# First MLP of a two-layer trunk: half 1 of its input turned once per token block, the Strassen-like forms made behind the turn

## The chip, the cores and the metric

The kernel runs on one core of one Trainium2 chip. The metric is the time of one execution on the device in microseconds (us). Before the change three runs gave 2055.06, 2055.20 and 2062.24 us; the median is 2055.2 us. Lower is better.

## The reference

The input x has 1024 tokens of 1024 channels in float32. There are two layers. The first mixes tokens with a gated linear recurrence, the second with a causal convolution; each mixer is followed by a layer norm, an MLP with squared ReLU and another layer norm. Cut to the place that matters here, the end of the first mixer and the first MLP:

```python
for i in range(DEPTH):
    ...
    x = layer_norm(DEEPNORM_ALPHA * x + mix, ln_mix_g[i], ln_mix_b[i])
    ff = jnp.square(jax.nn.relu(x @ ffn_w1[i])) @ ffn_w2[i]
    x = layer_norm(DEEPNORM_ALPHA * x + ff, ln_ffn_g[i], ln_ffn_b[i])
```

ffn_w1 is 1024 x 4096 and ffn_w2 is 4096 x 1024. The change concerns how x, the output of the first layer norm, is brought into the shape in which the product with ffn_w1 takes it.

## The kernel before

**Precision.** Every float32 operand is split into a high part (rounded to fp32r by a copy) and a low part (the rest), and a product is three matmuls, high x high, high x low and low x high (`product`, line 335). `split` (line 1042) makes the parts: a ScalarE copy for the high one, a VectorE subtraction for the low one.

**Seven products for eight.** The large products go by a scheme with seven products of half-sized blocks. The tokens are cut in two halves of 512 (half 0 and 1) and the channels in two halves of 512 (k = 0 and 1). Write x00, x10 for half 0 and channels 0 or 1, and x01, x11 for half 1. The MLP then needs seven forms of its input, kept transposed (channels on the partitions) and split, in `xf[1]` to `xf[7]` (line 1144): form 1 is x00, 2 is x10, 3 is x11, 5 is x00 - x01, 7 is x11 - x01, 6 is -(form 5) - x11 and 4 is -(form 6) - x10. `forms_of` (line 1119) makes forms 5, 6, 7 and 4 from four blocks. Seven forms of each weight block go with them; `Forms.unit` (line 130) loads four raw tiles of 128 x 1024 and makes the weights' forms from them in the order of `ORDER` (line 45): 1, 2, 6, 5, 7, 3, 4.

**The stage of the change (lines 1132 to 1178).** The output projection of the first mixer is computed block by block: four blocks t of 128 tokens in each half, two column halves n each, 24 matmuls a product. VectorE adds each product to y (`y[half]`, the residual), and behind n = 1 `x1_block` (line 1154) normalises the block. For half 0 two background jobs ("chores") turn the block: `turn` (line 1096) transposes four 128 x 128 pieces on TensorE into one PSUM bank of the ring `aux` (banks 3 and 4) and splits them from there into `xf[1]` and `xf[2]`. For half 1 `forms_of` makes tiles t for forms 5 and 6 (ring `ts`, two tiles of 2 KB per partition at 200 and 202 KB) and for form 4 (ring `t4s`, 212 to 218 KB) while tokens are still on the partitions, and each form is turned and split on its own. `keep` (line 1104) stores y to DRAM for the residual after the MLP. `x1_late` (line 1417) does what is left, form 3 and form 7 (ring `t7s` at 48 and 50 KB), during the first products of the MLP.

**The first MLP (lines 1411 to 1445).** Four early products (`up.form` at lines 1426 to 1430: the first two forms of the weight blocks c = 0 and c = 1) take weights that are loaded ahead (`early`, line 1141). Then the loop over c takes forms from `fw` (line 1413): weight slots at 144, 152, 48, 112 and 120 KB, raw tiles at 192, 196, 200 and 204 KB, sums at 160 and 164 KB. `Up` (line 1186) keeps squared ReLU outputs in `hr` at 168 and 176 KB and their forms in `ht` at 184 to 190 KB.

**What sets the order.** A chore is popped by every `product` (line 342, `bg.chore`). All buffers are views of one space at addresses written out in KB, so a view waits until those that lie there before it are free. Up to line 1038 the order on every engine is the one of the program; behind it the queues are ordered by the scheduler of the tile framework with its own timeline (line 1920), so the order in the trace differs from the program's in places.

Of the kernel before, what the change touches and what calls it, by code (L numbers as in the profile page):

```python
# [8 lines left out]
F32 = mybir.dt.float32  # L9
# [3 lines left out]
ALU = mybir.AluOpType  # L13
PSUM = bass.MemoryType.PSUM

P = 128
D = 1024
# [3 lines left out]
HT = 512  # L21
NTB = HT // P
# [141 lines left out]
class LateForms(Forms):  # L164

    turned = True
# [102 lines left out]
def body(ctx, tc, d, out):  # L269
    nc = tc.nc  # L270
# [9 lines left out]
    def view(kb, shape, dt=F32, name="t"):  # L280
        at, top = int(kb * 1024), KBYTES * 1024
        if at < edge[0]:
            if edge[0] < top:
                space.tile([P, (top - edge[0]) // 4], F32, name="gap")
            edge[0] = 0
        if at > edge[0]:
            space.tile([P, (at - edge[0]) // 4], F32, name="gap")
        edge[0] = at + (prod(shape) + 7) // 8 * 32
        return space.tile([P, *shape], dt, name=name)

    def ring(kbs, shape, name, dt=F32):
        return Ring([view(kb, shape, dt, name) for kb in kbs])

    def run(kb, n, size):
        return [kb + i * size for i in range(n)]

    def slots(kbs, name):
        return ring(kbs, (2, 1024), name, F32R)

    def raws(kbs, name="raw"):  # L300
        return ring(kbs, (1024,), name)
# [21 lines left out]
    bg = Background()  # L323
    vector = Clocked(nc.vector, bg.dve, vector_cost)
    tensor = Clocked(nc.tensor, bg.pe, tensor_cost)
# [6 lines left out]
    def aux():  # L332
        return rings["aux"]().rearrange("p (a b) -> p a b", a=NTB)
# [40 lines left out]
    ident = cst.tile([P, P], F32, name="ident")  # L374
    wide_t, rows = (HT,), (NTB, P)

    XF, VS, VO = {}, {}, {}
    x00, x10, x01, x11, t6 = [view(kb, (4, HT), F32, "xr") for kb in run(112, 5, 8)]
# [663 lines left out]
    def split(hi, lo, ps, scale=None):  # L1042

        if scale is None:
            nc.scalar.copy(out=hi, in_=ps)
            vector.tensor_tensor(out=lo, in0=ps, in1=hi.bitcast(F32), op=ALU.subtract)
        else:
            nc.scalar.activation(hi, ps, AF.Copy, scale=scale)
            vector.scalar_tensor_tensor(out=lo, in0=ps, scalar=scale, in1=hi.bitcast(F32), op0=ALU.mult, op1=ALU.subtract)
# [7 lines left out]
    def gain(kb, name, layer):  # L1057
        return vec(kb, f"{name}_g", layer), vec(kb + 4, f"{name}_b", layer)
# [12 lines left out]
    def moments(yt):  # L1071
        bs = stat.tile([P, 2, 6], F32, tag="bs", name="bs")
        for j in range(2):
            half_stats(bs, yt, j)
        mv = rstd_of(bs)
        return mv[:, 0:1], mv[:, 3:4]
# [14 lines left out]
    def norm(yt, g, b):  # L1091
        mu, rs = moments(yt)
        vector.scalar_tensor_tensor(out=yt, in0=yt, scalar=mu, in1=g, op0=ALU.subtract, op1=ALU.mult)
        vector.scalar_tensor_tensor(out=yt, in0=yt, scalar=rs, in1=b, op0=ALU.mult, op1=ALU.add)

    def turn(yt, xt, t, k0, nk):

        for k in range(0, nk, 4):
            pt = aux()
            for j in range(4):  # L1100
                tensor.transpose(pt[:, j, :], yt[:, (k0 + k + j) * P : (k0 + k + j + 1) * P], ident)
            split(xt[:, 0, k : k + 4, t * P : (t + 1) * P], xt[:, 1, k : k + 4, t * P : (t + 1) * P], pt)

    def keep(half, t, src):
        nc.sync.dma_start(out=kept[half][t], in_=src)
# [10 lines left out]
    def blocks(name, layer, c):  # L1116
        return [d[name][layer, c, q] for q in range(4)]

    def forms_of(x, out, only=(5, 6, 7, 4)):

        t = {i: out(i) for i in only}
        if 5 in only:
            vector.tensor_tensor(out=t[5], in0=x[0][0], in1=x[0][1], op=ALU.subtract)
            vector.scalar_tensor_tensor(out=t[6], in0=t[5], scalar=-1.0, in1=x[1][1], op0=ALU.mult, op1=ALU.subtract)
        if 7 in only:
            vector.tensor_tensor(out=t[7], in0=x[1][1], in1=x[0][1], op=ALU.subtract)
        if 4 in only:
            vector.scalar_tensor_tensor(out=t[4], in0=t[6], scalar=-1.0, in1=x[1][0], op0=ALU.mult, op1=ALU.subtract)
        return t
# [3 lines left out]


    g, b = gain(192, "ln_mix", 0)
    y = [view(160 + 16 * h, (NTB, D), F32, "y") for h in range(2)]
    for half in range(2):
        for t in range(NTB):
            nc.sync.dma_start(out=y[half][:, t], in_=d["x"][half * HT + t * P : half * HT + (t + 1) * P])
    ts, t4s = ring(run(200, 2, 2), wide_t, "t"), ring(run(212, 4, 2), wide_t, "t4")  # L1140
    early = [Slots(nc, vector, slots((204,), "fw"), raws((0,))), Slots(nc, vector, slots((112, 120), "fw"), raws((96, 100)))]
    early.append(Slots(nc, vector, slots((144,), "fw"), raws((152,))))

    xf = {i: view(kb, (2, 4, HT), F32R, f"x1f{i}") for i, kb in ((6, 0), (5, 16), (3, 32), (1, 64), (2, 80), (7, 96), (4, 128))}
    early[0].plan(blocks("w1q", 0, 0)[:1])
    early[1].plan([blocks("w1q", 0, 0)[1], blocks("w1q", 0, 1)[0]])
    early[2].plan(blocks("w1q", 0, 1)[1:2])
    yb = [[[y[n][:, t, k * HT : (k + 1) * HT] for n in range(2)] for k in range(2)] for t in range(NTB)]
    tt = {}

    def x1_form(t, i, src=None, k=0):
        turn(tt[t][i] if src is None else src, xf[i], t, k, 4)

    def x1_block(half, t):
        norm(y[half][:, t, :], g, b)
        if half == 0:
            bg.chores += [lambda: x1_form(t, 1, y[0][:, t, :]), lambda: x1_form(t, 2, y[0][:, t, :], 4)]
            return
        tt[t] = forms_of(yb[t], lambda i: (t4s if i == 4 else ts)(), (5, 6, 4))
        keep(0, t, y[0][:, t, :])  # L1160
        if t < NTB - 1:
            bg.chores += [lambda: x1_form(t, 6), lambda: x1_form(t, 5)]

    for half in range(2):
        for t, n in early_out + ((0, 1), (1, 1), (3, 0), (2, 1), (3, 1)) if half == 0 else [(t, n) for t in range(NTB) for n in range(2)]:
            ps = acc()
            if half or (t, n) not in early_out:
                product(ps, wide(oT[half], t, ws[n]))
            yv = y[half][:, t, n * HT : (n + 1) * HT]
            vector.scalar_tensor_tensor(out=yv, in0=yv, scalar=ALPHA, in1=ps, op0=ALU.mult, op1=ALU.add)  # L1170
            if n == 1:
                if half == 1 and t == 0:
                    early[0].ahead(1)
                x1_block(half, t)
                if half == 0 and t:
                    bg.chore()
# [232 lines left out]
            nc.sync.dma_start(out=raw, in_=d[name][at])  # L1409
            staged.append((name, at))  # L1410

    t7s = ring((48, 50), wide_t, "t7")
    fw = Forms(nc, vector, slots((144, 152, 48, 112, 120), "fw"), raws(run(192, 4, 4)), raws(run(160, 2, 4), "sum"), spare, 3, range(44))
    fw.todo = [[(blocks("w1q", 0, c), 2 if c < 2 else 0)] for c in range(NFC)]
    up = Up()

    def x1_late(t):
        turn(y[1][:, t, :], xf[3], t, 4, 4)
        tt[t].update(forms_of(yb[t], lambda i: t7s(), (7,)))
        x1_form(t, 7)  # L1420
        keep(1, t, y[1][:, t, :])

    late_forms = [lambda t=t: x1_late(t) for t in range(NTB)]
    bg.chores += [lambda: None] + late_forms[:1] + [lambda: x1_form(NTB - 1, 6), lambda: x1_form(NTB - 1, 5)] + late_forms[1:]
    bg.chores += [lambda t=t: x1_form(t, 4) for t in range(NTB)]
    up.form(0, 1, early[0].take(1)[0])
    up.form(0, 2, early[1].take(1)[0], late=True)
    up.form(1, 1, early[1].take(1)[0], ring((208, 210), wide_t, "c1"))
# [19 lines left out]
    y = [view(32 + 16 * h, (NTB, D), F32, "y") for h in range(2)]  # L1448
    fw = Slots(nc, vector, slots([112, 120, 144, 152, 128, 136, 168], "dw"), raws([192, 196, 200, 204, 160, 164], "dr"), spare, 6, range(10, 50))
    fh = Slots(nc, vector, slots([0, 8, 16, 24, 96, 104, 176], "dh"))  # L1450
    g, b = gain(184, "ln_ffn", 0)
# [61 lines left out]
    taken, turned, gate, normed = [0], [0], [None, [], None], [0]  # L1513
# [306 lines left out]
    y = [view(kb, (NTB, D), F32, "y") for kb in (88, 112)]  # L1820
    g, b = gain(184, "ln_ffn", 1)
# [102 lines left out]
```

## Time and profile before

| What | Value |
| --- | --- |
| Median of three runs | 2055.2 us |
| Span of the profiled execution | 2068.3 us |
| TensorE busy | 2031.0 us, 98% |
| VectorE busy | 1482.9 us, 72% |
| ScalarE busy | 1090.2 us, 53% |
| GpSimd busy | 388.4 us, 19% |
| Mean granted TensorE clock | 0.997 |
| Transposes of 128 x 128 between 440 and 570 us | 112 |
| First matmul of the first MLP (`ps<-x1f,fw`) | 519.7 us |

The profiled execution is one run of its own with a span of 2068.3 us from the first to the last instruction; nothing of the execution lies around that span in the trace, and it is longer than the median of the three timed runs. In a row of the profile, PE is TensorE's matmuls, PEld its weight loads, DVE VectorE, ACT ScalarE, POOL GpSimd and SPq the queue of SyncE, which issues DMA transfers. `out<-in` names the tiles written and read: ps is PSUM, x1f the seven forms `xf`, fw the weight forms, ident the identity matrix of a transpose, y the residual blocks, t the form tiles, raw and sum the raw weights and their sums. The bracket at the end of a timeline row gives how long the engine was idle before it and what ended that. A row with xN merges N instructions that follow each other.

### The profile page before, as it was taken

The numbers are of one execution on the slowest core, as the hardware profiler recorded it, in microseconds if no ns is written. First come the engines' busy times: TensorE is split into PE (matmuls) and PEld (weight loads), VectorE is DVE, ScalarE is ACT, GpSimd is POOL, SyncE is SP. The second block draws the span as 40 slices with busy tenths as digits, with TensorE's granted clock in tenths as the row PEclk, the third lists the DMA queues.
The fourth block names the chain that finished last, engine by engine and source line by source line (L and its number), as shares of the span: only waits on it lengthen the run. The fifth ranks groups of instructions, "written<-read, shape, count | busy, mean of one in ns | idle before, by whom it ended". The sixth has DMA issues, their size and how long they took to land. (4 is left out here: it accounts for less than half of the span.)

```text
span 2068.3 us, 29719 instructions
## 1 busy us (share of the span) xinstructions
PE 2031.0 (98%) x11192; PEld 1674.5 (81%) x11192; DVE 1482.9 (72%) x1976; ACT 1090.2 (53%) x1727; POOL 388.4 (19%) x387
## 2 busy tenths in 40 slices
PE   8999999999999999999999999999999999999998
PEld 7888777788888888888888888888878878888886
DVE  8698877877775666565567898889589666755556
ACT  5456555641464555444444776488625555343333
POOL 0112222111001000000001699079210000100002
PEclk9999999999999999999999999999999999999999
DMA  4778889852689786999998855587759778996542
GB/s 186 224 195 233 238 224 270 254 189 81 187 288 298 243 295 221 353 341 332 335 349 292 309 193 185 190 323 271 256 215 339 245 232 291 386 292 204 193 155 102
DMA packets 183944, 517.55 MB, mean 250 GB/s; under 512 B 17912, under 2 KB 49784, under 8 KB 182776
## 3 DMA queue, kind: packets, MB, share of 16 engines
q1 hardware_dynamic: 168312, 456.93, 62.6%
q0 software_dynamic: 15488, 58.72, 12.3%
q8 instruction: 87, 1.43, 0.3%
q14 instruction: 57, 0.47, 0.1%
HBM read 380.85 MB, written 201.85 MB: 282 GB/s over the span
## 5 line engine op out<-in xcount | busy, mean ns | idle before, releaser
L204 PE MATMUL ps<-dw,dh 128*128 128x512 f32 x2688 | 611.6, 389 | 1.9 <-ACT dh L72 1.1
L204 PEld LDWEIGHTS ps<-dw,dh 128*128 128x128 f32 x2688 | 504.1, 188 | 107.2 <-ACT dh L72 1.6
L204 PE MATMUL ps<-x1f,fw 128*128 128x512 f32 x1344 | 309.3, 390 | 2.3 <-DVE c L204 1.2
L204 PEld LDWEIGHTS ps<-x1f,fw 128*128 128x128 f32 x1344 | 251.1, 188 | 56.2 <-ACT c L1224 2.3
L204 PE MATMUL ps<-xf,fs 128*128 128x512 f32 x1008 | 249.3, 398 | 4.1 <-issue 1.9
L204 POOL TENSOR_TENSOR cb<-cb,prod 128x512 f32<-128x512 f32 x168 | 222.7, 1334 | 12.9 <-ACT prod L1555 2.3
L204 DVE TENSOR_TENSOR dh<-dh 128x1024 fp32r<-128x1024 f32 x112 | 136.4, 1222 | 117.3 <-ACT dh L72 117.1
L204 PEld LDWEIGHTS ps<-xf,fs 128*128 128x128 f32 x1008 | 184.5, 189 | 43.4 <-issue 2.1
L204 DVE SCALAR_TENSOR_TENSOR ps<-u,par,ps 128x512 f32<-128x512 f32 x296 | 206.2, 750 | 11.0 <-ACT ps L1567 9.5
L72 ACT CAST dh<-dh 128x1024 fp32r<-128x1024 f32 x112 | 117.4, 1051 | 163.7 <-DMA dh<-hf 163.7
L204 PE MATMUL ps<-xa,wa 128*128 128x512 f32 x864 | 203.1, 392 | 0.1
L204 PEld LDWEIGHTS ps<-xa,wa 128*128 128x128 f32 x864 | 160.3, 188 | 33.3 <-ACT ha L1289 0.3
L204 DVE TENSOR_TENSOR dw<-dr,dw 128x1024 fp32r<-128x1024 f32 x112 | 136.2, 1222 | 66.6 <-ACT dw L72 65.9
L72 ACT CAST dw<-dr 128x1024 fp32r<-128x1024 f32 x112 | 117.0, 1051 | 119.2 <-PE ps L204 100.2
L1555 ACT ACTIVATE prod<-u,par 128x512 f32<-128x512 f32 x168 | 119.8, 726 | 36.6 <-POOL cb L204 35.7
L518 POOL TENSOR_TENSOR mv<-mv,nhalf 128x1 f32<-128x1 f32 x32 | 43.3, 1355 | 407.6 <-DVE mv L204 407.6
L1408 POOL COPY next<-ss 128x1 f32<-128x1 f32 x38 | 21.2, 558 | 413.8 <-DVE spare L204 265.1
L204 PE MATMUL ps<-xb,wa 128*128 128x512 f32 x384 | 91.1, 393 | 0.0
L204 PE MATMUL ps<-w,oT 128*128 128x512 f32 x384 | 89.5, 391 | 1.3 <-ACT oT L932 0.8
L204 DVE TENSOR_TENSOR spare<-next,spare 128x1024 fp32r<-128x1024 f32 x38 | 46.5, 1224 | 60.6 <-ACT spare L1401 60.5
L204 PE MATMUL ps<-vw,xf 128*128 128x512 f32 x336 | 79.8, 399 | 6.0 <-ACT vw L435 5.2
L204 PEld LDWEIGHTS ps<-w,oT 128*128 128x128 f32 x384 | 71.5, 188 | 16.6 <-ACT oT L932 1.2
(236 smaller groups left out, 2959.6 us busy)
## 6 DMA issues: line engine op xcount, KB each, us to landing
wa<-ready SPq DMA_DIRECT2D x140, 512.0 KB, 5.5
dh<-hf SPq DMA_DIRECT2D x112, 512.0 KB, 5.3
sum_w<-in_w_dram POOLq DMA_DIRECT2D x40, 1024.0 KB, 10.9
ready<-spare SPq DMA_DIRECT2D x76, 512.0 KB, 4.6
raw<-in_w1q_dram SPq DMA_DIRECT2D x66, 512.0 KB, 4.4
dr<-sum_w SPq DMA_DIRECT2D x64, 512.0 KB, 5.7
hf<-ht SPq DMA_DIRECT2D x112, 256.0 KB, 4.9
dr<-in_w_dram SPq DMA_DIRECT2D x48, 512.0 KB, 5.3
```

The source lines that it names most:

```text
L72: self.nc.scalar.copy(out=slot[:, 0, c], in_=raw[:, c])
L204: return op(*args, **kw)
L518: nc.gpsimd.tensor_tensor(out=dst, in0=src, in1=nhalf[:, :n], op=ALU.pow)
L1408: nc.gpsimd.tensor_copy(out=raw[:, :1], in_=now)
L1555: nc.scalar.activation(tp, u[:, k : k + HT], AF.Copy, scale=tap(j, k))
```

## The change

Half 1's block is turned as it is, once: four transposes per channel half, eight per block. The forms are then made from the turned block in PSUM and from `xf[1]` and `xf[2]`, whose high and low parts are added up again.

- `x1_first` turns channels 0 of a block of half 1 (x01) and makes form 5 from `xf[1]` high, the turned block and `xf[1]` low; it splits it, and leaves x01 in its PSUM bank.
- `x1_second` turns channels 1 (x11), makes and splits form 6, copies x11 out of PSUM into `late_x[3]`, makes form 7 into `late_x[7]`, and form 4 into `late_x[4]`.
- `x1_late` splits forms 3, 7 and 4 from there, two channel groups of all 512 tokens (128 x 1024) at a time: six wide splits. They are chores of their own behind three empty ones, so that the first comes with the fourth early product.
- The two halves of y change places (half 0 at 176, half 1 at 160 KB); `late_x[3]` and `late_x[7]` take half 0's place at 176 and 184 KB once it is turned, `late_x[4]` takes 212 to 220 KB. `t4s` and `t7s` go. `keep` is called behind the norm for every block.

```diff
-    y = [view(160 + 16 * h, (NTB, D), F32, "y") for h in range(2)]
+    y = [view(160 + 16 * h, (NTB, D), F32, "y") for h in range(2)][::-1]
...
-    ts, t4s = ring(run(200, 2, 2), wide_t, "t"), ring(run(212, 4, 2), wide_t, "t4")
+    ts = ring(run(200, 2, 2), wide_t, "t")
+    late_x = {4: view(212, (4, HT), F32, "x4")}
...
-    def x1_form(t, i, src=None, k=0):
-        turn(tt[t][i] if src is None else src, xf[i], t, k, 4)
+    def of(x, t, i=slice(None)):
+        return x[..., t * P : (t + 1) * P] if i == slice(None) else x[:, i, :, t * P : (t + 1) * P]
+
+    def turned(yt, k0):
+        pt = aux()
+        for j in range(4):
+            tensor.transpose(pt[:, j, :], yt[:, (k0 + j) * P : (k0 + j + 1) * P], ident)
+        return pt
...
+    def x1_first(t):
+        s, pt = ts().rearrange("p (a b) -> p a b", a=4), turned(y[1][:, t, :], 0)
+        less(s, of(xf[1], t, 0).bitcast(F32), pt)
+        vector.tensor_tensor(out=s, in0=s, in1=of(xf[1], t, 1).bitcast(F32), op=ALU.add)
+        x1_split(5, t, s)
+        temp[t], x01[t] = s, pt
+
+    def x1_second(t):
+        s, pt = ts().rearrange("p (a b) -> p a b", a=4), turned(y[1][:, t, :], 4)
+        minus_both(s, temp[t], pt)
+        nc.scalar.copy(out=of(late_x[3], t), in_=pt)
+        less(of(late_x[7], t), of(late_x[3], t), x01[t])
+        x1_split(6, t, s)
+        x4 = of(late_x[4], t)
+        minus_both(x4, s, of(xf[2], t, 0).bitcast(F32))
+        less(x4, x4, of(xf[2], t, 1).bitcast(F32))
+
+    def x1_late(i, k):
+        split(xf[i][:, 0, k : k + 2], xf[i][:, 1, k : k + 2], late_x[i][:, k : k + 2])
...
     def x1_block(half, t):
         norm(y[half][:, t, :], g, b)
+        keep(half, t, y[half][:, t, :])
...
-        tt[t] = forms_of(yb[t], lambda i: (t4s if i == 4 else ts)(), (5, 6, 4))
-        keep(0, t, y[0][:, t, :])
+        if t == 0:
+            bg.done()
+            late_x.update({i: view(kb, (4, HT), F32, "xl") for i, kb in ((3, 176), (7, 184))})
         if t < NTB - 1:
-            bg.chores += [lambda: x1_form(t, 6), lambda: x1_form(t, 5)]
+            bg.chores += [lambda: x1_first(t), lambda: x1_second(t)]
...
-    t7s = ring((48, 50), wide_t, "t7")
...
-    late_forms = [lambda t=t: x1_late(t) for t in range(NTB)]
-    bg.chores += [lambda: None] + late_forms[:1] + [lambda: x1_form(NTB - 1, 6), lambda: x1_form(NTB - 1, 5)] + late_forms[1:]
-    bg.chores += [lambda t=t: x1_form(t, 4) for t in range(NTB)]
+    bg.chores += [lambda: None, lambda: x1_first(NTB - 1), lambda: x1_second(NTB - 1)] + [lambda: None] * 3
+    bg.chores += [lambda i=i, k=k: x1_late(i, k) for i in (3, 7, 4) for k in (0, 2)]
```

`split`, `turn`, `norm` and `keep` are unchanged; `minus_both(out, x, y)` is -x - y, `less` is x - y.

More of the change, by code (lines that the diff above doesn't have):

```diff
@@ L1147, in body @@
     early[2].plan(blocks("w1q", 0, 1)[1:2])
-    yb = [[[y[n][:, t, k * HT : (k + 1) * HT] for n in range(2)] for k in range(2)] for t in range(NTB)]
-    tt = {}
-    def x1_form(t, i, src=None, k=0):
-        turn(tt[t][i] if src is None else src, xf[i], t, k, 4)
+    temp, x01 = {}, {}
+    def of(x, t, i=slice(None)):
[5 more added lines that the diff above has]
+        return pt
@@ new lines, in less, with minus_both, x1_split @@
+    def less(out, x, y):
+        vector.tensor_tensor(out=out, in0=x, in1=y, op=ALU.subtract)
+    def minus_both(out, x, y):
+        vector.scalar_tensor_tensor(out=out, in0=x, scalar=-1.0, in1=y, op0=ALU.mult, op1=ALU.subtract)
+    def x1_split(i, t, src):
+        split(of(xf[i], t, 0), of(xf[i], t, 1), src)
+    def x1_first(t):
[4 more added lines that the diff above has]
+        temp[t], x01[t] = s, pt
@@ L1154, in x1_block @@
     def x1_block(half, t):
         norm(y[half][:, t, :], g, b)
+        keep(half, t, y[half][:, t, :])
         if half == 0:
-            bg.chores += [lambda: x1_form(t, 1, y[0][:, t, :]), lambda: x1_form(t, 2, y[0][:, t, :], 4)]
+            bg.chores += [lambda k=k: turn(y[0][:, t, :], xf[1 + k // 4], t, k, 4) for k in (0, 4)]
             return
-        tt[t] = forms_of(yb[t], lambda i: (t4s if i == 4 else ts)(), (5, 6, 4))
-        keep(0, t, y[0][:, t, :])
+        if t == 0:
+            bg.done()
+            late_x.update({i: view(kb, (4, HT), F32, "xl") for i, kb in ((3, 176), (7, 184))})
@@ L1415, in body @@
     up = Up()
[L1417 to L1421, printed above, removed]
-    late_forms = [lambda t=t: x1_late(t) for t in range(NTB)]
-    bg.chores += [lambda: None] + late_forms[:1] + [lambda: x1_form(NTB - 1, 6), lambda: x1_form(NTB - 1, 5)] + late_forms[1:]
-    bg.chores += [lambda t=t: x1_form(t, 4) for t in range(NTB)]
+    bg.chores += [lambda: None, lambda: x1_first(NTB - 1), lambda: x1_second(NTB - 1)] + [lambda: None] * 3
+    bg.chores += [lambda i=i, k=k: x1_late(i, k) for i in (3, 7, 4) for k in (0, 2)]
     up.form(0, 1, early[0].take(1)[0])
```

## The prediction

> **What bounds the kernel now.** I read the page's head first, then the granted clock, then TensorE's waits, then TensorE's timeline around the stage that the diff touches.
>
> ```profile
> span 2068.3 us, 29719 instructions
> PE 2031.0 (98%) x11192; PEld 1674.5 (81%) x11192; DVE 1482.9 (72%) x1976; ACT 1090.2 (53%) x1727; POOL 388.4 (19%) x387
> ```
> ```profile
> core 0: 2068.3 us, clock 0.997
> ```
> TensorE is busy 98% of the span at a clock of 0.997, so the clock is not in play, and 37 us of TensorE idle is all that waits can cost. An edit shortens the kernel only by taking instructions off TensorE or by closing part of those 37 us. The stage of the diff lies near a quarter of the span:
>
> ```profile
> core 0: us, PE busy (x) PEld busy (x) DVE busy (x) ACT busy (x) POOL busy (x), PEclk, DMA share, GB/s
> 500.00:520.00 20.00, 20.00 (x98) 16.76 (x97) 14.77 (x22) 2.34 (x4) 1.45 (x1) 1.00 0.30 93
> 520.00:540.00 20.00, 20.00 (x98) 16.65 (x97) 13.95 (x21) 10.23 (x16) 1.45 (x1) 1.00 0.49 170
> 540.00:560.00 20.00, 19.01 (x98) 15.73 (x97) 15.67 (x18) 10.86 (x18) 1.26 (x1) 1.00 0.71 212
> 560.00:580.00 20.00, 20.00 (x94) 16.32 (x94) 15.51 (x18) 11.35 (x18) 1.67 (x2) 1.00 0.82 193
> ```
> Here TensorE rests once, for about 1 us between 540 and 560; VectorE is busy 14 to 16 of 20 us and ScalarE at most 11. Behind 600 us the view of waits lists eleven reasons for which TensorE rests, the largest and the smallest being
>
> ```profile
> PE ps L204 <- ACT dh L72: 1.1, 1, 1.1
> PE ps L204 <- ACT z L1634: 0.2, 1, 0.2
> ```
> so none is over 1.1 us, all of them are under 12 us, and what is won at 500 to 570 us should reach the end.
>
> **What the change takes from TensorE.** Only the transposes of this stage:
>
> ```profile
> L204 PE MATMUL ps<-ident,t 128*128 128x128 f32 x64 | 9.3, 272 | 0.0
> L204 PE MATMUL ps<-ident,y 128*128 128x128 f32 x48 | 6.5, 272 | 0.0
> ```
> (The lines view from 440 to 570 us.) Before, every one of four token blocks has four transposes for each of the forms 6, 5, 7 and 4, made from tiles t (the 64), and for form 3 from y of half 1 (16 of the 48; the other 32 are half 0's and stay). After, a block of half 1 takes eight, four per half of D. So 64 + 16 become 32: 48 fewer. What one costs is not its 272 ns, which overlap, but the distance between starts:
>
> ```profile
> 495.39 1.03 PE L204 MATMUL ps<-ident,t 128*128 128x128 f32 x8
> 496.18 11.14 PE L204 MATMUL ps<-w,oT 128*128 128x512 f32 x48
> ...
> 526.17 0.60 PE L204 MATMUL ps<-ident,y 128*128 128x128 f32 x4
> 526.61 0.60 PE L204 MATMUL ps<-ident,t 128*128 128x128 f32 x4
> 526.96 8.20 PE L204 MATMUL ps<-x1f,fw 128*128 128x512 f32 x35
> ...
> 542.15 2.30 PE L204 MATMUL ps<-x1f,fw 128*128 128x512 f32 x9
> 545.43 3.91 PE L204 MATMUL ps<-x1f,fw 128*128 128x512 f32 x16 [0.99 <-DVE c L204]
> ...
> 558.45 0.60 PE L204 MATMUL ps<-ident,t 128*128 128x128 f32 x4
> 558.81 2.80 PE L204 MATMUL ps<-x1f,fw 128*128 128x512 f32 x11
> ```
> Eight delay the next matmul by 496.18 - 495.39 = 0.79 us, four by 558.81 - 558.45 = 0.36 us: 0.09 to 0.10 us each, so 48 are 4.3 to 4.7 us; I take 4.5. [...]
>
> In the timeline, 24 of the 80 transposes of half 1 stand before 519 us (24 also afterwards, of y instead of t), 24 between 526 and 545 (eight afterwards, the last block's) and 32 behind 545 (none afterwards). So 16 go ahead of the rest at 545.43, 1.5 us, and 32 behind it, 3.0 us.
>
> **What it adds to VectorE and ScalarE.** From the same lines view:
>
> ```profile
> L204 DVE TENSOR_TENSOR x1f<-ps,x1f 128x512 fp32r<-128x512 f32 x26 | 17.0, 681 | 11.2 <-ACT x1f L1045 11.2
> L204 DVE TENSOR_TENSOR fw<-raw,fw 128x1024 fp32r<-128x1024 f32 x6 | 7.2, 1214 | 1.7 <-ACT fw L72 1.7
> L204 DVE SCALAR_TENSOR_TENSOR t<-t,y 128x512 f32<-128x512 f32 x8 | 5.5, 683 | 0.0
> L204 DVE TENSOR_TENSOR t<-y 128x512 f32<-128x512 f32 x8 | 5.4, 687 | 0.1
> ```
> A block had four form operations and five split subtractions, nine of about 0.685 us. It gets three (first half) and five (second half), eight, with three of PSUM-reading and the rest of plain operands; the rows of both kinds agree (681 and 687 ns), so I price them alike. The six wide splits, 128x1024, are 1.21 us each. VectorE: 36 x 0.685 = 24.7 us before, 32 x 0.685 + 6 x 1.21 = 29.2 after, 4.5 more. In the loop over half 1, five operations per block become eight, 2.1 us more in a block of 507.16 - 495.39 = 11.77 us, of which VectorE now uses some 8.7 (14.77 of 20): 10.8 of 11.77. It fits, with 1 us left, so TensorE keeps its pace there, but the block's normalisation ends later. Behind 545 us the wide splits (7.3 us) replace some nine narrow ones (6.2 us): no difference. ScalarE gets three copies per block instead of five, and six wide ones of 1.05 us: about 1.6 us more on an engine that is half idle.
>
> **Edits that I cost at nothing.** The swapped places of y's halves and the earlier stores of kept:
>
> ```profile
> 423.36 6.54 SPq L1139 DMA_DIRECT2D y<-in_x_dram  x5
> 446.43 1.37 DVE L204 SCALAR_TENSOR_TENSOR y<-y,ps 128x512 f32<-128x512 f32 x2 [2.80 <-PE ps L204]
> ```
> y's last load leaves SyncE's queue at 429.9 us and its first reader runs at 446.43, after TensorE; half 0's new place is that of the recurrence's last tiles, free by then, so 16 us of matmuls cover it; without that cover a late load costs what it is late. The stores of kept are the same eight issues of 0.3 to 0.4 us, put behind each norm, and are read only by the down projection.
>
> **The wait that decides.** At 542.9 us (545.43 - 0.99 - 1.5) TensorE will be through with the four early products and wants the forms of the first full unit. All but one need raw[2] of four raw tiles. It lies at 200 KB (line 1413), over both t buffers (200 and 202, line 1140), so its load waits until t is free:
>
> ```profile
> 526.85 1.29 DVE L204 SCALAR_TENSOR_TENSOR y<-y,mv,ln_mix_b 128x1024 f32<-128x1024 f32 x1 [0.44 <-POOL mv L518]
> ...
> 528.65 1.28 DVE L204 TENSOR_TENSOR x1f<-ps,x1f 128x512 fp32r<-128x512 f32 x2
> ...
> 530.45 0.68 DVE L204 TENSOR_TENSOR c<-c,ps 128x512 f32<-128x512 f32 x1
> 531.05 1.41 DVE L204 SCALAR_TENSOR_TENSOR t<-t,y 128x512 f32<-128x512 f32 x2
> ...
> 540.06 1.22 DVE L204 TENSOR_TENSOR sum<-raw 128x1024 f32<-128x1024 f32 x1 [2.44 <-DMA raw<-in_w1q_dram]
> ```
> ```profile
> 536.30 6.47 SPq L135 DMA_DIRECT2D raw<-in_w1q_dram  x2
> ```
> ```profile
> 535.67 0.60 PE L204 MATMUL ps<-ident,t 128*128 128x128 f32 x4
> ```
> ```profile
> 535.63 1.26 ACT L1045 CAST x1f<-ps 128x512 fp32r<-128x512 f32 x2 [0.53 <-PE ps L204]
> ...
> 541.32 1.06 ACT L72 CAST fw<-sum 128x1024 fp32r<-128x1024 f32 x1 [1.63 <-DVE sum L204]
> ```
> Now: the last norm ends at 528.14, the t tiles that are turned are made by 531.7, the last transposes read them at 535.67 and after, until 536.27; the load leaves at 536.30, VectorE starts on it at 540.06 (3.76 later, having idled for it), ScalarE's cast of the sum ends at 542.4. From issue to usable weights are 6.1 us. Today TensorE then still has 2 us of product left, so this chain is just hidden.
>
> After: the norm ends at 528.1 plus 0 to 2.4 us (eight operations of block 2 where two splits and two seventh forms stood, some of them in gaps); I take 529.3. TensorE takes transposes up to 4 us behind their input (531.7 to 535.67 above): 3.5, so 532.8. But now t is read by VectorE, not TensorE, and is free only after the seventh of the block's eight operations: 0.4 for the transposes, 7 x 0.6 (two in 1.28, one in 0.68, so one every 0.6), one ScalarE copy between (0.6), two additions of early products ahead (1.3), 6.5 us, so 539.3. Issue, load, sum and cast: 539.4 + 6.1 = 545.5, against 545.43 today. The bounds: with the norm at 528.1, TensorE at once and nothing between, t is free at 533.3, the weights come at 539.5 and TensorE doesn't wait for them, so the restart is at 542.9; with the norm at 530.5 and 4 us to the transposes it is at 541.1 + 6.1 = 547.2. I expect TensorE to wait 2.6 us there: the 1.5 us of the 16 transposes and the old 0.99 us of rest become one longer wait.
>
> **Sum.** Ahead of the restart 0.0 (from -2.5 to +1.8), behind it -3.0: -3.0 us (-5.5 to -1.2) on the profiled span, 2068.3 to 2065.3. The runs shown have a median of 2055.2, 0.6% below that span, with the highest at 2062.24; the same 3.0 us, 0.15%, come off: 2052.2. A measurement of this kernel can tell about 0.5%, 10.3 us, from no change, so this would read as the same.
>
> **Rivals.**
> (A) The wait is hidden and all of it is won: 4.5 + 1.0 = 5.5 us, 2049.7. For it: slot 48 of the weight ring is no longer shared with the seventh forms' tiles, so the third form comes sooner. Against it: the load at 536.30 was already bare for 2.44 us on VectorE.
> (B) Slower than before: the same chain, but t is held so long that the restart comes after 548.4 us, where it has eaten the 3.0 us behind it as well; from there the kernel is a us slower for each us. If VectorE falls behind by 1 us in each of the loop's four blocks, the norm ends at 533.3, t is free at 543.3 and the restart at 549.5: 2056.3. With three of the wide splits ahead of the first sums, 3.6 us more: 2059.9. For it: VectorE at 10.8 of 11.77 us. Against it: TensorE rested nowhere in that loop, and its products have six PSUM banks (line 1132) to run ahead in.
> (C) A transpose costs TensorE its whole record: 48 x 0.272 = 13.1 us, 2042.1. Against it: eight of them in 0.79 us. [...]
> (D) Behind line 1038 the queues' orders are made anew by the planner of line 1920. A new order elsewhere can add or close rests; the bounds are the 37 us of idle and a like amount of new waits. Nothing speaks for a side, but a new wait is easier to make than an old one to close at 98%.
>
> **How the numbers follow.** Forecast 0.55; A 0.18; B 0.14, of which 0.03 beyond 10.3 us; C 0.05; D 0.08, of which 0.02 faster and 0.05 slower by over 0.5%. Faster by over 0.5%: C and D's part, 0.07. Slower: 0.03 + 0.05 = 0.08. The same: 0.85. The range holds forecast, A and B: from 2047.7 (A, less 2 us for the spread between runs) to 2059.9; C, D and B's tail, 0.16, lie outside. The forecast's own range is 2049.7 to 2054.0.
>
> **What would show it.** Right: 64 transposes of y from 440 to 570 us and none of t; a rest of TensorE of 2 to 3 us after the early products, with the load of raw[2] leaving at 539 to 540 us; no transposes behind it; TensorE's busy time lower by about 4 us. A rest under 1 us says A, one over 5 us B, a gap of 0.27 us between transposes C. My steps are wrong if TensorE rests inside the loop over half 1, or if the load of raw[2] isn't what the restart waits for.

## The result, and the profile after

The change makes the kernel slower: 2065.35 us (median of nine runs, 2062.97 to 2071.13) against 2058.1 us for the kernel before on the same chip (nine runs, 2055.06 to 2062.24), a ratio of 1.0035 (95% interval 1.0023 to 1.0047). A second comparison gave 2070.33 against 2062.75 us, 1.0034 (1.0020 to 1.0048). So 7 us were lost where 3.0 were to be won, and the time lies above the whole range of the prediction (2047.7 to 2059.9 us). The loss is under the 0.5% that the prediction took as its bound, but both intervals leave no change out.

The head of the page and the clock of the kernel after:

```profile
span 2063.6 us, 29615 instructions
PE 2025.6 (98%) x11144; PEld 1670.0 (81%) x11144; DVE 1487.9 (72%) x1978; ACT 1092.0 (53%) x1725; POOL 388.0 (19%) x387
```
```profile
core 0: 2063.6 us, clock 0.997
```
The span is shorter than the 2068.3 us of before, and TensorE is busy 5.4 us less (0.3 us less in a second pair of profiles; busy time was longer where the clock was low: four matmuls took 2.07 us at a granted clock of 0.50, in rows below, and 1.20 us at 1.00, at 540.36 us of the profile with held splits and a filled rest). Yet the kernel is slower. In the profiled execution of before the clock fell to one half twice, 3.4 us each time, long ahead of the stage. One of these stretches, from the windows of before (the third number from the right is the granted clock):

```profile
272.70:275.90 3.20, 2.60 (x120) 2.27 (x124) 1.53 (x4) 3.20 (x8) 0.00 (x0) 0.50 1.05 186
```
The kernel before reaches the first matmul of the first MLP at 519.72 us, the kernel after at 510.23. Spans can't be compared then; times from a common mark can. I take that first matmul (`ps<-x1f,fw`) as zero, "the mark", and number the 1344 matmuls of this form in the trace; the time that they take is "the up phase". "The restart" is matmul n = 96, the first behind the four early products.

The same windows as before, for the kernel after:

```profile
500.00:520.00 20.00, 20.00 (x98) 16.68 (x97) 19.63 (x28) 7.68 (x11) 2.90 (x2) 1.00 0.52 157
520.00:540.00 20.00, 15.51 (x69) 12.19 (x67) 17.13 (x22) 13.73 (x19) 0.00 (x0) 0.95 0.44 154
540.00:560.00 20.00, 17.63 (x65) 13.69 (x65) 14.54 (x14) 7.18 (x9) 2.13 (x2) 0.79 0.86 224
```
TensorE's busy time (second number) is 4.5 and 2.4 us short of its windows, VectorE is busy 19.63 of 20 us between 500 and 520, and the clock falls to 0.95 and 0.79. TensorE's timeline says where:

```profile
524.44 0.60 PE L204 MATMUL ps<-ident,y 128*128 128x128 f32 x4
524.79 0.48 PE L204 MATMUL ps<-x1f,fw 128*128 128x512 f32 x1
525.11 0.60 PE L204 MATMUL ps<-ident,y 128*128 128x128 f32 x4
525.46 8.21 PE L204 MATMUL ps<-x1f,fw 128*128 128x512 f32 x35
538.17 2.07 PE L204 MATMUL ps<-x1f,fw 128*128 128x512 f32 x4 [4.49 <-ACT fw L72]
542.41 2.07 PE L204 MATMUL ps<-x1f,fw 128*128 128x512 f32 x4 [2.17 <-ACT fw L72]
544.68 5.62 PE L204 MATMUL ps<-x1f,fw 128*128 128x512 f32 x16 [0.20 <-DVE fw L204]
```
Where before rested once for 0.99 us, it now rests three times, 6.86 us, for weight forms: twice for their cast on ScalarE (line 72) and once, 0.20 us, for a low half made by VectorE. The transposes are as forecast, none of t:

```profile
L204 PE MATMUL ps<-ident,y 128*128 128x128 f32 x64 | 8.8, 272 | 0.0
```
What the weight forms waited for stands in the queues of SyncE, VectorE and ScalarE:

```profile
530.37 0.33 SPq L135 DMA_DIRECT2D raw<-in_w1q_dram  x1
```
```profile
514.76 1.28 DVE L204 SCALAR_TENSOR_TENSOR y<-y,mv,ln_mix_b 128x1024 f32<-128x1024 f32 x1
...
532.59 2.35 DVE L204 TENSOR_TENSOR x1f<-xl,x1f 128x1024 fp32r<-128x1024 f32 x2
534.86 1.22 DVE L204 TENSOR_TENSOR sum<-raw 128x1024 f32<-128x1024 f32 x1
536.00 0.68 DVE L204 TENSOR_TENSOR c<-c,ps 128x512 f32<-128x512 f32 x1
536.60 2.35 DVE L204 TENSOR_TENSOR x1f<-xl,x1f 128x1024 fp32r<-128x1024 f32 x2
538.87 1.22 DVE L204 TENSOR_TENSOR x1f<-x,x1f 128x1024 fp32r<-128x1024 f32 x1
540.00 1.22 DVE L204 TENSOR_TENSOR sum<-sum,raw 128x1024 f32<-128x1024 f32 x1
```
```profile
530.35 3.89 ACT L1045 CAST x1f<-xl 128x1024 fp32r<-128x1024 f32 x4
534.14 1.99 ACT L1045 CAST x1f<-x 128x1024 fp32r<-128x1024 f32 x2
536.04 0.62 ACT L1235 ACTIVATE c<-c 128x512 f32<-128x512 f32 x1
536.57 0.61 ACT L1236 ACTIVATE hr<-c 128x512 f32<-128x512 f32 x1
537.09 1.03 ACT L72 CAST fw<-sum 128x1024 fp32r<-128x1024 f32 x1
...
541.31 1.04 ACT L72 CAST fw<-sum 128x1024 fp32r<-128x1024 f32 x1 [2.66 <-DVE sum L204]
```
VectorE's first row is the end of the last block's norm, to which I come back. The load of raw[2] leaves at 530.37, 20.14 us from the mark (before: 536.30, 16.58). VectorE does two wide splits ahead of the first sum. That sum is ready at 536.08, but ScalarE has six wide casts and two activations ahead of its cast. The second sum comes only at 540.00, because VectorE does three wide splits first.

The start of matmul number n, in us from the mark, in the profiles of this study. The last row is the ratio of the timed runs to those of the kernel before. The columns from "raw order" on are the experiments below; "spare" is the edit of the last two:

```
n       before (two)    after (two)     raw     held    both    both+   after+
                                        order           edits   spare   spare
96      25.71  25.75    27.94  27.95    24.43   26.33   24.58   24.58   27.95
120     32.16  32.20    39.92  39.39    29.99   34.72   30.15   30.15   38.95
240     62.34  62.69    67.12  66.59    58.31   62.45   59.70   59.53   66.18
600    143.94 144.29   148.72 148.19   140.37  144.05  141.30  141.13  147.78
840    200.63 198.69   207.83 205.68   200.10  204.43  198.09  195.59  202.18
1343   314.87 312.70   321.84 319.72   314.11  318.49  312.13  309.61  316.19
ratio  1               1.0035 1.0034   0.9993  1.0004  0.9990  0.9969  1.0009
```
In the first pair the loss is 2.2 us at the first rest (n = 96), 5.5 more by n = 120, minus 3.0 by n = 240 (no more transposes), and 2.4 again between 600 and 840; the end gives back 0.2, which leaves 7.0 us. Both pairs give 7.0; the timed runs give 7.3 and 7.6.

### The profile page after: what moved, and what is told of

Its sections match the earlier page's. It is cut to its first block, busy times and chain, and to the rows that moved or that the text cites. A ratio compares the mean times of both kernels' runs of the same rounds, so it can differ in the third digit from the quotient of the medians.

```text
span 2063.6 us, 29615 instructions
## 1 busy us (share of the span) xinstructions
PE 2025.6 (98%) x11144; PEld 1670.0 (81%) x11144; DVE 1487.9 (72%) x1978; ACT 1092.0 (53%) x1725; POOL 388.0 (19%) x387
## 5 line engine op out<-in xcount | busy, mean ns | idle before, releaser
L1235 ACT ACTIVATE c<-c 128x512 f32<-128x512 f32 x72 | 45.0, 629 | 83.8 <-DVE c L204 83.8
```

The lines of the kernel that those rows point to most:

```text
L1235: nc.scalar.activation(t, src, AF.Relu, scale=scale)
```

## The experiments

My theory after the trace was that raw[2]'s load, held by t, sets the restart, and that the wide splits stand ahead of the weight forms; the rivals were the held PSUM bank, the clock, and a loss elsewhere.

**raw order: the block that both sums need goes into a tile that t does not cover.**

```diff
-    fw = Forms(..., raws(run(192, 4, 4)), ...)
+    fw = Forms(..., raws((192, 200, 196, 204)), ...)
```


> The four raw buffers of the first MLP's weights are handed out in another order (192, 200, 196, 204 instead of 192, 196, 200, 204), so that the block which both sums need is loaded into a buffer that t does not cover, and the block over t is one that was already over t before. If the restart hangs on the load that waits for t: that load leaves some 13 us earlier, the rests of 4.49 and 2.17 us in the changed kernel both fall under 1 us, the granted clock stays at 1.00 between 538 and 548 us, and the time falls by about 6 (rests) + 3.9 (half clock) = 10 us, to 2054 to 2057 us. If the rests come from the six wide splits ahead of the weight forms alone, a rest of 2 to 3 us stays and the time is 2060 to 2063 us. If the loss lies elsewhere, nothing changes: 2065 us.

2060.91 us, ratio to before 0.9993 (0.9983 to 1.0003). The load leaves by 7.13 us from the mark instead of 20.14 (the first of three in the row is the last that doesn't wait for t), and the restart has no rest over 1 us:

```profile
521.19 16.31 SPq L135 DMA_DIRECT2D raw<-in_w1q_dram  x3
```
```profile
538.49 6.63 PE L204 MATMUL ps<-x1f,fw 128*128 128x512 f32 x28 [0.98 <-DVE c L204]
545.95 6.41 PE L204 MATMUL ps<-x1f,fw 128*128 128x512 f32 x27 [0.82 <-DVE fw L204]
```
By n = 600 it is 3.6 us ahead of before: the forecast gain, and more. By n = 840 the lead is 0.5 us to before's first profile, and to its second it is 1.4 us behind. So the late load, and what stands around it, makes the loss at the restart; a second loss shows that I had not looked for.

**held: wide splits only behind the first formed weight.**

```diff
     def x1_late(i, k):
+        nc.gpsimd.tensor_copy(out=xf[i][:, 0, k, :1], in_=fw.slots.views[0][:, 1, :1])
```


> Each of the six wide splits waits for the low half of the first formed weight (a one-column copy on GpSimd from it into the split's output), so that none of them stands ahead of the casts of the two sums on ScalarE and VectorE; loads as in the changed kernel. If the load waiting for t sets the restart and the wide splits only add to it: the cast of the first sum starts where its sum is ready (536.1 instead of 537.1 us in the profile of the changed kernel), the first rest falls from 4.49 to 3 to 3.5 us and the second from 2.17 to under 0.6, the time to 2058 to 2063 us according to whether the clock still falls to one half. If the wide splits alone make the rests, both go: 2054 to 2057 us. If they have no part in it, 2065 us.

2062.94 us, 1.0004 (0.9992 to 1.0016). One rest is left at the restart, and the clock is at one half from just before its end on:

```profile
541.25 14.46 PE L204 MATMUL ps<-x1f,fw 128*128 128x512 f32 x50 [2.88 <-ACT fw L72]
```
```profile
540.50:547.10 6.60, 5.85 (x14) 4.34 (x15) 6.60 (x7) 3.33 (x4) 1.88 (x2) 0.50 1.01 341
```
The load leaves 20.14 us from the mark, as in the kernel after, and n = 96 comes at 26.33: 6.2 us from issue to use, the prediction's chain. So of the first rest the wide splits are 1.6 us (27.94 to 26.33) and the late load the other 2.9, and the second rest is theirs alone.

**A third PSUM bank for the transposes.**

```diff
-    rings["mm"] = bank((0, 1, 2, 5, 6, 7))
+    rings["mm"], rings["aux"] = bank((0, 1, 2, 5, 6)), bank((3, 4, 7))
```


> A third PSUM bank for the transposes (taken from the six of the products), so that the bank which x01 holds from one block's first transposes to its second ones no longer keeps the next block waiting. If the last block's transposes are late because of that held bank (524.4 us, 8.4 us behind the end of their norm), they come some 3 us earlier, and with them t's release, the load and the restart: first rest about 1.5 us instead of 4.49, time 2058 to 2062 us. If the bank is not what they wait for, or the products miss their sixth bank, 2065 us or more.

2068.38 us, 1.0025 (1.0009 to 1.0040). The last block's transposes start 14.08 us from the mark instead of 14.21 (530.91 less 516.83, where the mark lies in this run):

```profile
530.91 1.03 PE L204 MATMUL ps<-ident,y 128*128 128x128 f32 x8
531.70 2.98 PE L204 MATMUL ps<-x1f,fw 128*128 128x512 f32 x12
537.14 4.60 PE L204 MATMUL ps<-x1f,fw 128*128 128x512 f32 x12 [2.46 <-DVE xl L204]
```
They are behind about 60 matmuls in TensorE's order either way; the bank theory falls. The products now rest 2.46 us until VectorE has read a turned block (xl) out of its bank. Bank 7 is one of those that `Up` gives to the MLP's products, which the edit leaves as it is, so this is likely a wait for a shared bank.

**The first rest filled with work.** Twenty matmuls whose result nothing reads:

```diff
     up.form(1, 2, early[2].take(1)[0], late=True)
+    for _ in range(20):
+        nc.tensor.matmul(banks[:, 3], xf[1][:, 0, 0, :P], xf[2][:, 0, 0], start=True, stop=True)
```


> Twenty matmuls more (128x512, old operands, into a bank that is not read) stand ahead of the restart, about 4.6 us, so that TensorE works through the rest of 4.49 us; nothing else changes, and their result is used nowhere. If that rest is what trips the clock to one half (538.1 to 548.3 us), the clock stays at 1.00 at least until the second rest of 2.17 us and the time falls by up to 3.9 us, to 2061 to 2063 us, with the restart where it was. If the half clock comes from the second rest, or costs nothing, 2065 us. If the fillers themselves end behind the operands, up to 2067 us.

2072.03 us, 1.0041 (1.0028 to 1.0054): no gain.

```profile
537.98 4.70 PE L1461 MATMUL ps<-x1f,x1f 128*128 128x512 f32 x20
542.65 1.19 PE L204 MATMUL ps<-x1f,fw 128*128 128x512 f32 x4
546.87 1.20 PE L204 MATMUL ps<-x1f,fw 128*128 128x512 f32 x4 [3.02 <-ACT fw L72]
```
The first rest is gone, the second grows from 2.17 to 3.02 us, and matmul 108 starts 36.33 us from the mark in both this kernel and the kernel after. Up to there TensorE waits for weight forms whether the clock is whole or half.

**held, and its one rest filled.**

```diff
     def x1_late(i, k):
+        nc.gpsimd.tensor_copy(out=xf[i][:, 0, k, :1], in_=fw.slots.views[0][:, 1, :1])
...
+    for _ in range(13):
+        nc.tensor.matmul(banks[:, 3], xf[1][:, 0, 0, :P], xf[2][:, 0, 0], start=True, stop=True)
```

> The wide splits held, and thirteen matmuls more ahead of the restart (128x512, old operands, into a bank that is not read; their result is used nowhere), so that the one rest of 3.0 us that was left there is filled with work. If that rest trips the granted clock: it stays at 1.00 from 541 to 551 us, the 12 matmuls behind the restart take 2.7 us again instead of 5.4, and the time falls by about 2.9 us against the held kernel. If the fall of the clock has another cause: clock 0.5 as before, and no gain or a loss of up to 1 us.

2065.5 us, 1.0023 (1.0010 to 1.0037), against 1.0004 for held alone. The clock stays whole:

```profile
538.00:548.00 10.00, 9.40 (x40) 6.85 (x39) 8.85 (x9) 4.99 (x6) 2.65 (x7) 1.00 0.87 278
```
So the half clock came with that rest, in one profile of each kernel. But matmul 144 starts at 40.12 us from the mark and in held at 40.16: the 1.6 us won by n = 120 are spent waiting for the next form. My price of 2.9 us for the half clock falls; here it is nothing by n = 144. Why the timed runs are slower than those of held is not shown: in the profiles this kernel's up phase is the shorter one, 315.8 against 318.5 us.

**Both edits: raw order and held splits.**

```diff
-    fw = Forms(..., raws(run(192, 4, 4)), ...)
+    fw = Forms(..., raws((192, 200, 196, 204)), ...)
...
     def x1_late(i, k):
+        nc.gpsimd.tensor_copy(out=xf[i][:, 0, k, :1], in_=fw.slots.views[0][:, 1, :1])
```

> Both of the earlier edits: the raw buffers in the order 192, 200, 196, 204 and the wide splits held until a weight is formed. The first edit alone left no rest over 1.2 us at the restart and the clock at 1.00, so holding the wide splits has nothing left to remove there. If the late load was the cause and the wide splits only stretched it: the first 120 matmuls as with the first edit alone, time within 2 us of it (ratio to the kernel before 0.9985 to 1.0005). If the wide splits cost something by themselves: 2 to 5 us less than with the first edit alone.

2059.54 us, 0.9990 (0.9978 to 1.0001). n = 120 is as with the raw order alone (30.15 and 29.99), as the first theory has it. At n = 600 this kernel is 0.9 us behind the raw order, at n = 840 it is 2.0 ahead: that difference lies in the second loss. The times are not told apart (0.9990 and 0.9993).

**The second loss.** With the raw order alone, TensorE rests here, and ScalarE's and GpSimd's queues show why:

```profile
660.75 3.51 PE L204 MATMUL ps<-x1f,fw 128*128 128x512 f32 x9 [3.44 <-ACT c L1261]
```
```profile
653.67 0.57 ACT L1261 COPY c<-ps 128x512 f32<-128x512 f32 x1
658.22 1.04 ACT L1438 CAST spare<-next 128x1024 fp32r<-128x1024 f32 x1 [3.98 <-DMA next<-in_wpw_dram]
659.17 1.04 ACT L72 CAST fw<-raw 128x1024 fp32r<-128x1024 f32 x1
660.12 1.07 ACT L1261 COPY c<-ps 128x512 f32<-128x512 f32 x2
```
```profile
648.23 0.83 POOL L423 DMA_DIRECT2D sum_w<-sum_w  x1 [9.21 <-DMA hf<-hr]
648.77 0.48 POOL L1445 COPY next<-ss 128x1 f32<-128x1 f32 x1
```
The PSUM copies (line 1261) that free TensorE's banks stand behind a cast that waits 3.98 us for a load ahead, `next`: weights of a later stage, which the function `spare` loads, splits and stores during this MLP. For three in eight weight forms a one-column copy marks that the form is done (`ss<-fw`), and a second one (`next<-ss`, line 1445 in the kernel after) lets the next load ahead go. That second copy is on GpSimd, and stands there behind an addition in DRAM (`sum_w`) that GpSimd was kept 9.21 us from issuing.

**One load ahead skipped.**

```diff
-    fw = Forms(..., spare, 3, range(44))
+    fw = Forms(..., spare, 3, [m for m in range(44) if m != 24])
```


> The raw buffers in the order 192, 200, 196, 204, and one of the loads ahead for later stages skipped (that of the 24th formed weight; later ones take its place). With the raw order alone, a rest of 3.6 us stood 143 us behind the start of the up phase, where ScalarE waits in its queue for a load ahead (issued at 649.3, cast at 658.2 us) and the PSUM evacuations stand behind it. If the second loss is that wait: the rest there goes under 0.6 us and the up phase falls from 314.1 to 310.5 to 311.5 us, the time 2.5 to 3.6 us under that of the raw order alone (ratio to before 0.9975 to 0.9985). If the stretch is bound by the transfers as such, the rest comes back at a later load and the time does not change by over 1 us.

2063.82 us, 1.0013 (0.9998 to 1.0028); not told apart from the raw order alone. A rest of 2.65 us stands at the same place, behind a cast at the same place, of a load that was not skipped. So this run says nothing on the theory.

**The one-column copy on VectorE, throughout, with both edits.** Added to both edits:

```diff
-            nc.gpsimd.tensor_copy(out=raw[:, :1], in_=now)
+            nc.vector.tensor_copy(out=raw[:, :1], in_=now)
```


> Raw buffers in the order 192, 200, 196, 204, wide splits held, and the one-column copy that lets a load ahead go (next<-ss) on VectorE instead of GpSimd, whose queue stands behind the DRAM sums at that time (with the raw order alone: the count at 127.8 us behind the start of the up phase, the copy at 134.7, the load at 135.2, landed 144.1). If the second loss comes from the load being let go late: it leaves some 6 us earlier, ScalarE's wait for it shrinks, the rests between 140 and 205 us behind the start of the up phase fall from 1.4 (both edits) or 3.6 us (raw order) to under 1 us, up phase 311 to 312 us, ratio to before 0.998 to 0.9985. If the transfers are the bound: no change against both edits alone (0.999), the rests elsewhere.

2064.65 us, 1.0009 (0.9996 to 1.0023). The rests between 140 and 205 us are gone and the up phase takes 309.8 us, 2.3 less than with both edits; but behind the MLP, the way from the first matmul that reads tile xa (`ps<-xa,wa`) to the first that reads xb takes 97.2 us, against 93.6. The gain is given back there: TensorE waits 1.69 and 0.78 us for loads of wa, and the mean granted clock is 0.91 between 1133 and 1153 us. Whether the later loads' copies do this is tried below.

**The same copy alone in the kernel before.**

```diff
-            nc.gpsimd.tensor_copy(out=raw[:, :1], in_=now)
+            nc.vector.tensor_copy(out=raw[:, :1], in_=now)
```

> The kernel before with only that one-column copy on VectorE. It rests 1.8 us in all at the three places between 140 and 205 us behind the start of its up phase. If the load is let go late there too: these rests fall under 1 us, ratio 0.9993 to 0.9998. If the transfers are the bound: 1.000.

2067.04 us, 1.0021 (1.0010 to 1.0032): up phase 313.3 us (314.9 and 312.7 without), xa to xb 99.3 us against 92.9. The same trade, at a loss.

**The raw order alone in the kernel before.**

```diff
-    fw = Forms(..., raws(run(192, 4, 4)), ...)
+    fw = Forms(..., raws((192, 200, 196, 204)), ...)
```

> The kernel before with the raw buffers in the order 192, 200, 196, 204 and nothing else. Its own load of that block waits for t too, and its rest at the restart is 1.16 us. If the order is worth what that rest shows: 0.5 to 1.5 us less, ratio 0.9993 to 0.9998. If the gain of the order in the changed kernel is of another kind (some 8 us for any kernel): 0.996.

2064.99 us, 1.0017 (1.0005 to 1.0028): slower. The restart comes 1.16 us earlier (n = 96 at 24.55), and from n = 600 to 840 it loses 1.8 us to before's first profile and 4.1 to its second. A restart won is not a kernel won while the second wait stands.

**Both kernels once more, with no edit.** The kernel before, and the kernel after:

> The kernel before, unchanged, a second profile: whether the two half-clock stretches in its first 430 us and the rests in its up phase (1.16 us at the restart, 1.8 us between 140 and 205 us behind the start of the phase) come again. If they are its own: the same places and sizes within 0.3 us. If they come from when transfers land: the restart's rest again, the others elsewhere.

> The changed kernel, unchanged, a second profile and time on the same chip as the kernel before: rests of 4.7 and 2.6 us at the restart and half clock behind them again if their cause is the order of the work (the load behind t, the wide splits ahead of the weights); the rests 140 to 205 us behind the start of the up phase (4.2 us) again if the order makes them, 1 to 3 us if it is when transfers land. Ratio 1.002 to 1.005.

Before: span 2057.1 us, restart within 0.05 us of the first profile, no half clock but at the end of the span, and no rest from n = 600 to 840. After: the same rests of 4.50, 2.17 and 0.20 us and 10.24 us of half clock; from n = 600 to 840 it loses 3.1 us to an unbroken row of matmuls (54.4 us), 4.7 in the first profile; before lost 2.3 and nothing. So the restart is made by the order of the work, and the second loss varies by about 2 us from run to run and is larger after.

**Both edits, and the copy on VectorE in the first MLP's up phase alone.** Added to both edits:

```diff
-            nc.gpsimd.tensor_copy(out=raw[:, :1], in_=now)
+            (nc.vector if len(ready) < 13 else nc.gpsimd).tensor_copy(out=raw[:, :1], in_=now)
```


> Raw order 192, 200, 196, 204, wide splits held, and the copy that lets a load ahead go on VectorE for the first MLP's up phase alone (the first thirteen loads); later ones on GpSimd again. With the copy on VectorE throughout, the up phase took 309.8 us (both edits 312.1, the kernel before 314.9 and 312.7), and the two products behind the down phase some 4 us more (97.2 instead of 93.5 us from the first xa to the first xb product). If that loss belongs to the later loads' copies: up phase 309.5 to 311 us, xa to xb 93 to 94 us, ratio to before 0.997 to 0.9985. If the loss follows from the loads of the up phase: xa to xb 96 to 98 us, ratio 0.9995 to 1.001.

2057.85 us against 2063.5, ratio 0.9969 (0.9957 to 0.9981): faster than both kernels. Up phase 309.6 us, xa to xb 93.8 us; so the later loads' copies made the loss there. The copy now follows its mark at once, and TensorE's waits from the mark to the end of the phase are

```profile
642.35 0.15 DVE L1436 COPY ss<-fw 128x1 f32<-128x1 f32 x1
642.54 0.15 DVE L1446 COPY next<-ss 128x1 f32<-128x1 f32 x1
```
```profile
PE ps L204 <- ACT fw L72: 1.5, 2, 1.1
PE ps L204 <- ACT c L1262: 0.8, 1, 0.8
PE ps L204 <- DVE x1f L204: 0.2, 1, 0.2
```

**That copy in the kernel after, without the other edits.**

> The changed kernel with only that copy on VectorE for the up phase; restart as in the changed kernel (rests of 4.7 and 2.6 us, 10.24 us at half clock). If the loss 140 to 205 us behind the start of the up phase (2.4 and 0.8 us over the kernel before in two profiles) comes from loads let go late: up phase 317 to 319.5 us instead of 319.7 to 321.8, ratio 1.0015 to 1.003. If it follows from the restart alone: no change, 1.003 to 1.004.

2065.95 us against 2063.5, 1.0009 (0.9997 to 1.0020). TensorE's waits in the up phase are the restart's and no others:

```profile
PE ps L204 <- ACT fw L72: 6.7, 2, 4.5
PE ps L204 <- DVE fw L204: 0.2, 1, 0.2
```
So 0.26% goes, some 5 us with 3 to 4 us either way; the two profiles of the kernel after lose 4.7 and 3.1 us there. The sixteen profiles of this study agree: from n = 600 to 840 the four with the copy on VectorE take 54.4 to 55.1 us, and of the twelve with it on GpSimd one takes 54.4 and the others 56.7 to 60.4.

That is not all the change's doing, for the kernel before has such losses too. The same copy in both kernels compares like with like: their up phases are then 313.3 and 316.2 us, 2.9 apart, instead of 7.0. So by these profiles some 4 of the 7 us go with loads let go late and some 3 with the restart, less what the transposes bring. No run has the kernel before with the copy on VectorE in the up phase alone, so its timed runs can't be compared in this way.

## Why the prediction was wrong

- Right: 48 transposes fewer, none of t, and none behind the restart. A transpose costs TensorE far less than its 0.272 us (0.11 to 0.12, by the next point), so rival C falls.
- Mis-sized: what a transpose costs. From n = 120 to 240 before takes 30.18 us and after 27.20, an unbroken row. Only 24 of before's transposes lie there (eight at 555.97, four each at 558.45, 561.44, 565.54 and 567.37 us), and 0.15 us of the difference is a wait at n = 196, so one costs 0.11 to 0.12 us, not 0.09 to 0.10. The distance to the next matmul misses that the matmul behind that one is late too: it starts 314 to 316 ns later, where most of the others are 227 ns apart. By this the 48 are about 5.5 us (an estimate) and not 4.5. So more was to be won than forecast, not less.
- Right: TensorE does not rest in the loop over half 1, although VectorE is busy 19.63 of 20 us around its end.
- Right: the load of raw[2] is what the restart waits for, and t is free behind the seventh of the block's operations on VectorE (529.65 to 530.34 us). With the splits held, TensorE rests 2.88 us there, where 2.6 were forecast.
- Right by luck: when that load leaves. It was forecast for 539.4, 19.7 us from before's mark, and it left 20.14 us from the mark. But the last norm was forecast to end 9.6 us from the mark and ended at 5.8 (516.04), earlier than before's 8.4; and the transposes, forecast 3.5 us behind it, came 8.4 behind it, as they stand behind about 60 matmuls in TensorE's order. The two errors nearly cancel.
- Wrong, the step "Issue, load, sum and cast: 539.4 + 6.1 = 545.5". The 6.1 us are what the chain takes with the wide splits held (6.2). In the changed kernel it takes 7.8 us (530.37 to 538.17). VectorE starts the first sum 4.5 us behind the load's issue instead of 3.8, as two wide splits stand ahead of it, and ScalarE starts that sum's cast 1.0 us after it is ready, as its six wide casts and two activations come first. "Ahead of the restart 0.0 (from -2.5 to +1.8)" came out as +2.2 us at n = 96.
- Wrong, the step "Behind 545 us the wide splits (7.3 us) replace some nine narrow ones (6.2 us): no difference". They do not run behind the restart; they run from 530 to 543.5 us, on both engines that make the weight forms. I had priced their busy time and not asked whose queue they enter ahead of whom. This makes the second rest. By n = 120 the kernel is 7.8 us behind.
- "The clock is not in play": it was, 10.24 us of it, but what it took was small, up to 0.9 us from n = 108 to 120 (39.92 - 36.33 = 3.59 us in after; 38.95 - 36.21 = 2.74 with the late copy moved, where the same rests stand and these twelve matmuls start 228 ns apart).
- Wrong, the step "What is won at 500 to 570 us should reach the end". The waits behind 600 us were at most 1.1 us each in the one profile that was read, and the prediction put what they could grow to at nothing. From n = 600 to 840 the changed kernel loses 4.7 and 3.1 us where before lost 2.3 and nothing; the raw order alone, 3.6 us ahead at n = 600, lost 5.3.
- Of the rivals, B had the right mechanism in its last sentence ("three of the wide splits ahead of the first sums, 3.6 us more") and the wrong way to it: t was held only 0.5 us longer than forecast.

Left open: why loads let go late cost 3.1 to 4.7 us after and 0 to 2.3 before. It may be that the loads' place against TensorE's work moved; no run tests that.

## What to carry to other kernels

Work that is merged into wider pieces is to be priced by the queues that it enters: list what each engine does between the last load and the wait that ends the stage, and see what is behind the new piece (here the first sum's cast started 1.0 us after its sum was ready, behind six wide casts and two activations). Where a buffer becomes free late, give it to a block that is needed late (here the load left by 7.13 us from the mark instead of 20.14). A gain ahead of an engine that waits for loads can be given back there, as here (with the raw order, 3.6 us ahead at n = 600 and at n = 840 0.5 us ahead or 1.4 behind), so find that wait, and what lets its load go, before counting the gain to the end.

## What the hardware did that I had not expected

The granted clock was 0.50 for 10.24 us at the restart in both profiles of the kernel after, for some 6.8 us there with the splits held (a mean of 0.66 between 540 and 550 us), and twice for 3.41 us in before's first profile (the end of the span aside: 5.16 us in the kernel after, 5.93 in before's first profile). After's stretch, in its windows:

```profile
538.20:548.20 10.00, 7.63 (x16) 5.10 (x17) 9.83 (x9) 2.67 (x4) 1.26 (x1) 0.50 1.01 281
```
The half clock with the third bank:

```profile
537.50:540.70 3.20, 3.20 (x9) 2.49 (x8) 3.20 (x5) 3.20 (x5) 0.00 (x0) 0.50 0.96 360
```
That followed a rest of 2.46 us, while behind a rest of 2.65 us with one load skipped the clock was 1.00:

```profile
652.00:662.00 10.00, 7.35 (x32) 5.75 (x32) 5.39 (x5) 4.40 (x6) 0.00 (x0) 1.00 0.80 294
```
With the copy on VectorE throughout, TensorE rested 1.69 and 0.78 us between 1133 and 1153 us, and the mean clock there was 0.91. In these runs the length of a single rest does not tell whether the clock falls; what else decides is not shown.
